# Queries' projection handed out within the recurrence, and the output projection's recurrent half as float32 products

## The chip, the cores and the metric

The kernel runs on one NeuronCore of a Trainium2 chip. The metric is the device time of one execution in microseconds, as the median of the runs shown. Five instruction streams matter: PE (TensorE's matmuls, with PEld for its weight loads), DVE (VectorE), ACT (ScalarE), POOL (GpSimd) and SP (SyncE, which issues the DMAs). Each executes its own list in order; semaphores join them.

## The reference

One step of a streaming layer, for 1024 new frames of one stream and 16 frames for each of 8 running streams, 1152 rows in all, in 9 tiles of 128 rows. What the change touches is marked.

```python
h = rmsnorm(x, norm_mix)
proj = h @ w_in                                  # 1024 -> xr, gate, q, k, v, qi, ki, wi
xc = causal_conv(xr, ...)                        # 4 taps
r, i = sigmoid(xc @ w_rg + b_rg), sigmoid(xc @ w_ig + b_ig)      # 8 blocks of 64
a = exp(-8 * r * softplus(-lru_lambda))
hs = scan(h_t = a_t * h_{t-1} + sqrt(1 - a_t^2) * i_t * xc_t)    # the recurrence, 512 wide
y_a = hs * gelu(gate)
q = rope(rmsnorm(q per head, q_norm), pos)       # moved: 8 heads of 64
k = rope(rmsnorm(k per head, k_norm), pos)
# indexer: scores of qi, ki; top 256 keys of each row; attention over these -> y_b (512 wide)
x = x + concat(y_a, y_b) @ w_out                 # changed: y_a's half, rows 0 to 511 of w_out
hf = rmsnorm(x, norm_ffn)
x = x + (silu(gate part) * up part) @ w_ffn_out
```

All inputs and outputs are float32.

## The kernel before

The class `Kernel` writes the whole program in a chain of phases: norm of `x` with keys and values; indexer; recurrence (`lru`); queries' projection (`q_proj`); recurrent half of the output projection (`out_tile` with the key "wa"); attention; attention half of the output projection ("wb"); feed-forward.

*How products are made.* Most products are made in the type `fp32r`. For the sake of precision an operand is split there into a high and a low part (`split`, or `hi` and `lo`), and `mm3` issues three fast matmuls, high by high, high by low and low by high. `mm4` (L210) issues one true float32 matmul on unsplit operands; the trace shows it as two records of a weight load and a matmul each. The recurrence uses `mm4` for its convolution (`taps` by `xp`, four products added up) and its gates (`bd` by `xc`). All other projections use `mm3` (`mm`, L205).

*Order of the work.* Every piece is a Python generator, a "stream". `run` (L93) steps through `width` streams at a time in the order given, and besides through "side" streams, whenever its model of the engines' clocks says they are due. What comes out is an order for each engine; a scheduler behind it moves instructions once more, so the order of the program differs in many places whenever anything changes. All operations of DVE, ACT and POOL are recorded in one helper, L66, and are told apart by their tiles.

*The recurrence* goes through four columns of 128 channels. For each column `lru_main` projects the input (24 matmuls of 384 columns for each of three thirds of the rows), ACT copies it to `xp`, PE convolves it, ACT copies it to `xc`, PE makes the gates, ACT and DVE (`ti`, `tt`, `tr`) make the coefficients and DVE scans. `lru_gate` projects the column's gelu gate, and POOL multiplies it into `yF`, which holds `y_a` transposed, channel by row, in float32. Beside this the top-k search of the indexer runs as a side stream on DVE (`tk_cand`, `tk_cnt`, `jk`) and ACT (`jk`, passes over scores with a sum).

*Weights.* One stream, `loader`, loads weights in a list's order: DMA into one of two `raw` buffers, then a split into slots of 4 KB a partition in the pool `wr`; there are 8 slots (`SLOTS`). The recurrence's weights come first (two slots for each of eight, alternately main and gate, split on POOL), then two halves of the queries' weights (four slots each), then four rows of 128 of `w_out` ("wa"), the first two in slots and the others in spare room, each split by ACT and POOL (`load_wout`).

*Queries* (`q_tile`, L1197 on): a tile is 128 rows by half of the 512 columns, 24 matmuls of 256 columns; 18 tiles. ACT copies PSUM to `qn` and squares it head by head with a sum (`sq`, four instructions and four reads of the accumulator); then `rope`: DVE `qn` by `tab`, POOL `rp` twice, DVE adds. Nine rotation tables, multiplied by the gain on POOL, serve both halves. This phase begins when all streams of the recurrence have been handed out.

*Recurrent half of the output projection*: `out_prep` splits `yF` tile by tile into `rest` (ACT high, POOL low), `out_tile` loads `x` into `acc`, makes 24 matmuls of 512 columns for each of 9 tiles, and DVE adds PSUM into `acc`. As side streams, `k_rope` rotates the keys (`kn`, one table and one transpose for each tile) and `q_norm` scales the queries (POOL, `qss`).

Of the kernel before, what the change touches and what calls it, by code (L numbers as in the profile page):

```python
# [19 lines left out]
D = 1024  # L20
# [61 lines left out]
class Kernel:  # L82
# [10 lines left out]
    def run(self, streams, width, side=(), carry=()):  # L93
# [4 lines left out]
        act = list(carry)  # L98
# [6 lines left out]
        while todo or act:  # L105
            while todo and len(act) < width:
                act.append([self.clock, todo.pop()])
            self.clock = max([self.clock] + [b - self.QUEUE for b in self.busy.values()])
            for x in list(side):
                if due(x) <= self.clock:  # L110
                    lat = self.step(x[1])
                    if lat is None:
                        side.remove(x)
                    else:
                        x[0] = self.clock + lat
            x = next((a for a in act if a[0] <= self.clock), None)
            if x is None:
                x = min(act, key=lambda a: a[0])
                t = min([x[0]] + [due(a) for a in side])
                if t < x[0]:  # L120
                    self.clock = max(self.clock, t)
                    continue
                self.clock = x[0]
            self.pe0 = self.pe
            lat = next(x[1], None)
            self.clock = self.now()
            self.pe0 = self.pe
            if lat is None:
                act.remove(x)
            else:  # L130
                x[0] = self.clock + lat
# [132 lines left out]
    def build(self, upto=99):  # L264
# [61 lines left out]
        if upto < 3:  # L326
            return close()
        self.fence()
# [45 lines left out]
        with tc.tile_pool(name="wob", bufs=2, side=R) as tp:  # L374
# [3 lines left out]
            self.run([self.out_tile(i, "wb", tp, False) for i in range(NT)] + [self.ffn_start()], self.W_OUT,  # L378
                     [self.out_prep(False)] + side + [self.ffn_first()])
# [9 lines left out]
    YS_LO = ('pool', 'dve')  # L389
    C_FIRST = 2  # L390
# [9 lines left out]
    WA_HE = 'act'  # L400
# [3 lines left out]
    BD = 2  # L404
# [15 lines left out]
    def loader(self):  # L420
        I = self.I
        jobs = [("qi", 8, lambda n: self.load_512(1792, n))]
        jobs += [(("lru", n), 2, lambda n, c=c, n_=n: self.load_cols128(I["w_in"], c, n, self.LRU_HE[n_])) for n, c in enumerate(self.LRU_COLS)]
        jobs += [(("q", k), 4, lambda n, k=k: self.load_cols256(1024 + 256 * k, n)) for k in range(2)]
        jobs += [(("wa", c), 2 if c < 2 else 0, lambda n, c=c: self.load_wout([(0, c * 128, 128)], n, self.WA_HE, self.WA_LO[c]))
                 for c in range(4)]
# [601 lines left out]
    def lru_main(self, n, c, lp):  # L1028
# [14 lines left out]
        taps = lp.tile([128, 4, 128], F32, tag="taps", name="taps", bufs=2)  # L1043
# [148 lines left out]
    def q_proj(self, tp):  # L1192
        gq = self.load_g(tp, self.I["q_norm"], "gq")
        self.n_q, self.qtab = 0, {}
        return [self.q_tile(i, half, tp, gq) for half in range(2) for i in range(NT)]

    def q_tile(self, i, half, tp, gq):  # L1197
# [3 lines left out]
        if not half:  # L1201
            self.qtab[i] = self.tables(tp, i, gq, NT)
# [19 lines left out]
        self.rope(x, x, self.qtab[i], 4, tp)  # L1222
# [54 lines left out]
    WA_LO = ('pool', 'pool', 'pool', 'pool')  # L1277

    def load_wout(self, parts, n, he="act", le="pool"):

        t = self.raw.tile([128, D], F32, tag="raw", name="raw")
        for p0, r0, m in parts:
            self.nc.sync.dma_start(t[p0:p0 + m], self.I["w_out"][r0:r0 + m, :])
        ws = []
        yield from self.claim(n)
        while not n and self.spare is None:
            yield 0.3
        for q in range(2):
            w = self.wslot([2, 512]) if n else self.spare.pop(0).rearrange("p (x n) -> p x n", x=2)
            self.split(w, t[:, q * 512:(q + 1) * 512], he, le)  # L1290
            ws.append(w)
            yield 1.0
        return ws
# [21 lines left out]
    def out_prep(self, first):  # L1315

        self.ys = {}
        if first:

            while self.n_q < NT + 3:  # L1320
                yield 0.3
            self.rest = self.hblk.tile([128, 3 * D], F32R, tag="h", name="rest")
            acc = self.hblk.tile([128, 3, D], F32, tag="h", name="acc")
            self.acc = [acc[:, i] for i in range(3)]

            while self.n_q < NT + 6:
                yield 0.3
            self.smr = self.hblk.tile([128, 3 * D], F32R, tag="h", name="smr")
            self.spare = [self.smr[:, k * 1024:(k + 1) * 1024] for k in range(3)] + [self.rest[:, 2048:3072]]
        for i in range(NT):  # L1330
# [6 lines left out]
            self.lo(ys[:, 1], src, ys[:, 0], self.YS_LO[0 if first else 1])  # L1337
# [3 lines left out]
    def out_tile(self, i, key, tp, first):  # L1341
        nc = self.nc
        if first:
            nc.sync.dma_start(self.acc[i], self.x_src(i))
# [4 lines left out]
        early = first and i < self.C_FIRST  # L1349
        pos = [self.ps(), self.ps()] if early else [None, None]  # L1350
        for c in range(4) if early else ():
            w, = yield from self.wait_w((key, c))
            for q in range(2):
                self.mm3(pos[q], ys[:, 0, c, :], ys[:, 1, c, :], w[q][:, 0, :], w[q][:, 1, :], c == 0, c == 3)
            yield 0.0
        if first:
            w = yield from self.wait_w(*((key, c) for c in range(4)))
            if i == NT - 1:
                self.wused -= 4
        for q in range(2):  # L1360
            if not first:
                u, v = yield from self.wait_w((key, q, 0), (key, q, 2))
                if q and i >= NT - 2:

                    self.half_b += 1
                    while self.half_b < 2:
                        yield 0.2
            po = pos[q]
            if po is None:
                po = self.ps()  # L1370
                for c in range(4):
                    wc = w[c][q] if first else (u + v)[c]
                    self.mm3(po, ys[:, 0, c, :], ys[:, 1, c, :], wc[:, 0, :], wc[:, 1, :], c == 0, c == 3)
# [5 lines left out]
        if not first:  # L1379
            xs = tp.tile([128, D], F32, tag="xs", name="xs", bufs=3)  # L1380
            yield from self.norm_T(self.acc[i], xs, self.gf, self.hf[i // 3], (i % 3) * 128, tp)
            self.hf_done.add(i)
# [367 lines left out]
```

## Time and profile before

| | us |
|---|---|
| median of 3 runs (1585.16 to 1586.07) | 1585.86 |
| the profiled execution, its own time | 1582.82 |
| its span in the trace | 1580.7 |
| norm, keys, values | 0 to 76 |
| indexer | 76 to 186.5 |
| recurrence | 186.5 to 396.5 |
| queries' projection | 396.5 to 449.5 |
| recurrent half of the output projection | 449.5 to 513.3 |
| attention | to about 720 |
| its half of the output projection, feed-forward | to 1580 |

| | busy us | share |
|---|---|---|
| PE | 1477.3 | 93% |
| DVE | 886.4 | 56% |
| ACT | 624.4 | 39% |
| POOL | 288.7 | 18% |

The mean granted clock of TensorE is 0.969. The stages' ends are read from PE's timeline, at the first matmul of a stage. The chain of waits gives PE 72% of the span and DVE 15%. A row of the timeline gives start, length, engine, line, operation, tiles, shape and count of the merged instructions, and in brackets the engine's idle time before it and what ended it. Line numbers are those of the kernel before; in the changed kernel L205, L210 and L215 are L207, L212 and L217.

### The profile page before, as it was taken

To read this page: it belongs to the slowest core of one execution; us is meant where nothing else is said; L and a number is where in the kernel's file an instruction comes from. 1 tells how busy PE (TensorE), PEld (TensorE's weight loads), DVE (VectorE), ACT (ScalarE), POOL (GpSimd) and SP (SyncE) were. 2 spreads that over 40 slices of the span, in tenths; PEclk is the share of its full clock that TensorE was granted. 3 is DMA by queue.
4 is the path that set the end of the run, shared out by engine and by line. 5 is a ranking of instruction groups with operands and counts; after the bars stand their busy time and mean duration, and the time that the engine had idled before them with its cause. 6 is when DMAs were issued, how large, how long until landed. Compare 5 with 4: busy or idle time off the path is not lost.

```text
span 1580.7 us, 21030 instructions
## 1 busy us (share of the span) xinstructions
PE 1477.3 (93%) x7858; PEld 1335.3 (84%) x7858; DVE 886.4 (56%) x1909; ACT 624.4 (39%) x1484; POOL 288.7 (18%) x433
## 2 busy tenths in 40 slices
PE   6899898875989899999999999999999999999998
PEld 6777676764977688888999999999898989898987
DVE  7656899998676887768424242423333242424143
ACT  5447967867631987755312120202020202121100
POOL 5424223227484444400000000000000000000000
PEclk7999899988999899999999999999999999999999
DMA  7211110100140001120302020202020202111002
GB/s 241 66 32 42 35 29 16 29 14 14 44 156 0 8 14 47 48 67 28 94 14 67 14 75 6 80 1 80 1 80 0 81 18 63 30 51 52 29 1 120
DMA packets 93798, 74.66 MB, mean 47 GB/s; under 512 B 13236, under 2 KB 84532, under 8 KB 93696
## 3 DMA queue, kind: packets, MB, share of 16 engines
q1 hardware_dynamic: 93696, 73.32, 15.5%
q8 instruction: 62, 1.02, 0.3%
q14 instruction: 40, 0.33, 0.1%
HBM read 67.03 MB, written 6.27 MB: 46 GB/s over the span
## 4 chain that ended last, share of the span: by engine, by line
PE 72%; DVE 15%; ACT 5%; POOL 3%; issue 3%; DMA 1%; SPq 0%; POOLq 0%; ACTq 0%; DVEq 0%
PE ps L205 67%; DVE jk L66 7%; PE ps L215 3%; DVE tk_cand L66 2%; ACT jk L66 1%; DVE tr L66 1%; POOL rp L66 1%; PE ps L210 1%; DVE ti L66 1%; POOL qn L66 1%; DVE s L66 1%; ACT qeo L66 1%; ACT m L66 1%; ACT relu L66 0%; DMA tab<-in_rope_dram 0%
## 5 line engine op out<-in xcount | busy, mean ns | idle before, releaser
L205 PE MATMUL ps<-hf,w 128*128 128x384 f32 x2556 | 460.6, 338 | 0.0
L205 PEld LDWEIGHTS ps<-hf,w 128*128 128x128 f32 x2556 | 451.5, 187 | 0.8
L205 PE MATMUL ps<-w,a 128*128 128x512 f32 x999 | 239.1, 390 | 0.0
L66 DVE TENSOR_TENSOR acc<-ps,acc 128x512 f32<-128x512 f32 x234 | 161.3, 690 | 134.4 <-PE ps L205 133.9
L205 PEld LDWEIGHTS ps<-w,a 128*128 128x128 f32 x999 | 187.3, 188 | 40.1
L66 ACT ACTIVATE w<-raw 128x512 fp32r<-128x512 f32 x128 | 77.8, 630 | 303.0 <-PE ps L205 220.9
L66 DVE TENSOR_TENSOR sg<-ps,sg 128x384 f32<-128x384 f32 x66 | 36.7, 557 | 276.4 <-PE ps L205 275.9
L66 DVE TENSOR_TENSOR w<-raw,w 128x512 fp32r<-128x512 f32 x116 | 76.8, 687 | 87.4 <-ACT w L66 87.2
L66 ACT ACTIVATE jk<-s,tk_cand 128x384 bf16<-128x384 f32 (+3 forms) x128 | 99.4, 776 | 61.8 <-DVE tk_cand L66 53.0
L66 ACT ACTIVATE a<-sg 128x384 fp32r<-128x384 f32 x66 | 34.5, 523 | 217.9 <-DVE sg L66 217.9
L205 PE MATMUL ps<-hf,rest 128*128 128x384 f32 x612 | 114.5, 334 | 0.0
L205 PE MATMUL ps<-h,w 128*128 128x384 f32 x576 | 108.7, 347 | 0.5 <-ACT relu L66 0.5
L205 PEld LDWEIGHTS ps<-hf,rest 128*128 128x128 f32 x612 | 106.9, 188 | 0.2
L205 PEld LDWEIGHTS ps<-h,w 128*128 128x128 f32 x576 | 102.3, 190 | 4.7 <-ACT relu L66 0.6
L205 PE MATMUL ps<-w,h 128*128 128x256 f32 (+1 forms) x600 | 94.6, 314 | 0.6 <-DVE to L66 0.6
L205 PE MATMUL ps<-w,rest 128*128 128x512 f32 x324 | 83.0, 406 | 8.2 <-POOL rest L66 8.0
L205 PEld LDWEIGHTS ps<-w,h 128*128 128x128 f32 x600 | 82.2, 188 | 7.3 <-DVE to L66 0.9
L205 PEld LDWEIGHTS ps<-w,rest 128*128 128x128 f32 x324 | 61.3, 194 | 22.7 <-POOL rest L66 8.9
L66 ACT ACTIVATE sg<-ps 128x384 f32<-128x384 f32 x66 | 32.1, 486 | 122.0 <-PE ps L205 122.0
L210 PE MATMUL ps<-xp,taps 128*128 128x384 f32 (+2 forms) x128 | 44.5, 504 | 37.7 <-ACT xp L66 37.7
L210 PEld LDWEIGHTS ps<-xp,taps 128*128 128x128 f32 x128 | 26.7, 231 | 51.7 <-issue 43.8
L66 POOL TENSOR_SCALAR m<-m,mx 128x128 f32<-128x128 f32 (+7 forms) x64 | 47.6, 752 | 68.5 <-DVE mx L66 61.7
(261 smaller groups left out, 2185.2 us busy)
## 6 DMA issues: line engine op xcount, KB each, us to landing
raw<-in_w_ffn_in_dram SPq DMA_DIRECT2D x44, 512.0 KB, 4.9
raw<-in_w_ffn_out_dram SPq DMA_DIRECT2D x22, 512.0 KB, 3.5
raw<-in_w_in_dram SPq DMA_DIRECT2D x16, 512.0 KB, 3.8
out_dram<-acc SPq DMA_DIRECT2D x9, 512.0 KB, 2.6
x<-in_x_prompt_dram SPq DMA_DIRECT2D x8, 512.0 KB
acc<-in_x_prompt_dram SPq DMA_DIRECT2D x8, 512.0 KB, 9.1
tab<-in_rope_dram SPq DMA_DIRECT2D x34, 64.0 KB, 1.8
raw<-in_w_out_dram SPq DMA_DIRECT2D x4, 512.0 KB, 3.5
```

The costliest lines, as they stand in the source:

```text
L66: return f(*args, **kw)
L205: self.nc.tensor.matmul(out, lhsT, rhs, start=start, stop=stop)
L210: self.nc.tensor.matmul(out, lhsT, rhs, start=start, stop=stop)
L215: self.nc.tensor.transpose(out, in_, self.ident[0:n, 0:n])
```

## The change

- `run` takes a list `back` in place of `carry`: streams that are stepped only when no stream of the phase is ready, two of them at a time. `q_proj`'s 18 streams are made before the recurrence and passed as `back`; what is left of them runs in the queries' phase. Their memory now exists beside the recurrence's, and for that `bd` and `taps` have one buffer each instead of two, and the rotation tables three buffers instead of nine, so that each of the 18 tiles loads and multiplies its own.
- The loader brings the first half of the queries' weights after the third of the recurrence's eight weights, the second half after the eighth. The first half holds four of the eight slots until its ninth tile.
- The recurrent half of the output projection multiplies in float32: `load_wa` loads 128 rows of `w_out` into one slot, unsplit; `out_tile_a` issues `mm4` on `yF` and `wa`, 8 products of 512 columns for each of 9 tiles, 72 in place of 216 fast ones. The splits of `yF` (9 on ACT, 9 on POOL) and of these weights (8 and 8) are gone. `out_prep` is left to the attention half; its allocations are in `out_room`.

```diff
-    def run(self, streams, width, side=(), carry=()):
+    def run(self, streams, width, side=(), back=()):
...
-            x = next((a for a in act if a[0] <= self.clock), None)
+            x = next((a for a in act + list(back[:2]) if a[0] <= self.clock), None)
             if x is None:
-                x = min(act, key=lambda a: a[0])
+                x = min(act + list(back[:2]), key=lambda a: a[0])
...
-        with tc.tile_pool(name="lru", bufs=1, side=R) as tp:
-            self.phase = 1
-            side = self.run(self.lru(tp), 3, [self.lru_prep(tp)] + side)
...
         with tc.tile_pool(name="tq", bufs=2, side=R) as tp:
+            queries = [[self.clock, g] for g in self.q_proj(tp)]
+            with tc.tile_pool(name="lru", bufs=1, side=R) as lp:
+                self.phase = 1
+                side = self.run(self.lru(lp), 3, [self.lru_prep(lp)] + side, queries)
             self.phase = 2
-            prep, lo = self.out_prep(True), self.lru_out()
-            side = [x for x in self.run(self.q_proj(tp), 3, [prep, lo] + side) if x is not prep]
+            prep, lo = self.out_room(), self.lru_out()
+            side = [x for x in self.run([g for _, g in queries], 3, [prep, lo] + side) if x is not prep]
...
-            side = self.run([self.out_tile(i, "wa", None, True) for i in range(NT)], 2, [prep] + side + [kr, qr])
+            side = self.run([self.out_tile_a(i) for i in range(NT)], 2, [prep] + side + [kr, qr])
...
-    BD = 2
+    BD = 1
...
-        jobs += [(("wa", c), 2 if c < 2 else 0, lambda n, c=c: self.load_wout([(0, c * 128, 128)], n, self.WA_HE, self.WA_LO[c]))
-                 for c in range(4)]
+        lru = [(("lru", n), 2, lambda n, c=c, n_=n: self.load_cols128(I["w_in"], c, n, self.LRU_HE[n_])) for n, c in enumerate(self.LRU_COLS)]
+        q = [(("q", k), 4, lambda n, k=k: self.load_cols256(1024 + 256 * k, n)) for k in range(2)]
+        jobs += lru[:3] + q[:1] + lru[3:] + q[1:]
+        jobs += [(("wa", c), 1, lambda n, c=c: self.load_wa(c)) for c in range(4)]
...
-        taps = lp.tile([128, 4, 128], F32, tag="taps", name="taps", bufs=2)
+        taps = lp.tile([128, 4, 128], F32, tag="taps", name="taps", bufs=1)
...
-        if not half:
-            self.qtab[i] = self.tables(tp, i, gq, NT)
+        tab = self.tables(tp, i, gq, 3)
...
+    def load_wa(self, c):
+
+        yield from self.claim(1)
+        w = self.wr.tile([128, D], F32, tag="w", name="wa")
+        self.nc.sync.dma_start(w, self.I["w_out"][c * 128:(c + 1) * 128, :])
+        return w
...
+    def out_tile_a(self, i):
+
+        nc = self.nc
+        nc.sync.dma_start(self.acc[i], self.x_src(i))
+        w = []
+        pos = [self.ps(), self.ps()]
+        for c in range(4):
+            w += yield from self.wait_w(("wa", c))
+            for q in range(2):
+                self.mm4(pos[q], self.yF[:, c, i * 128:(i + 1) * 128], w[c][:, q * 512:(q + 1) * 512], c == 0, c == 3)
+            yield 0.0
+        if i == NT - 1:
+            self.wused -= 4
+        for q in range(2):
+            a = self.acc[i][:, q * 512:(q + 1) * 512]
+            nc.vector.tensor_tensor(a, pos[q], a, op=ALU.add)
+            yield 0.4 if q else 0.0
```

More of the change, by code (lines that the diff above doesn't have):

```diff
@@ L90, in __init__ @@
         self.nc = Engines(tc.nc, self)
-    def run(self, streams, width, side=(), carry=()):
+    def run(self, streams, width, side=(), back=()):
         todo = list(streams)[::-1]
-        act = list(carry)
+        act = []
         side = self.side = [[self.clock, g] for g in side]
@@ L128, in run @@
             if lat is None:
-                act.remove(x)
+                (act if any(x is a for a in act) else back).remove(x)
             else:
@@ L377, in build @@
             self.half_b, self.hf_done, self.w1_first, self.first_ps = 0, set(), [], {}
-            self.run([self.out_tile(i, "wb", tp, False) for i in range(NT)] + [self.ffn_start()], self.W_OUT,
-                     [self.out_prep(False)] + side + [self.ffn_first()])
+            self.run([self.out_tile(i, tp) for i in range(NT)] + [self.ffn_start()], self.W_OUT,
+                     [self.out_prep()] + side + [self.ffn_first()])
         yst.close()
@@ L388 @@
     LO_LAT = 15.0
-    YS_LO = ('pool', 'dve')
-    C_FIRST = 2
     WARM = 16
@@ L399 @@
     EXP_EARLY = False
-    WA_HE = 'act'
     WB_HE = 'act'
@@ L1193, in q_proj @@
         gq = self.load_g(tp, self.I["q_norm"], "gq")
-        self.n_q, self.qtab = 0, {}
+        self.n_q = 0
         return [self.q_tile(i, half, tp, gq) for half in range(2) for i in range(NT)]
@@ L1221, in q_tile @@
         x = x.rearrange("p (h d) -> p h d", h=4)
-        self.rope(x, x, self.qtab[i], 4, tp)
+        self.rope(x, x, tab, 4, tp)
     def q_norm(self, tp):
@@ L1274, in k_rope @@
             yield 2.0
[L1277 to L1293, printed above, removed]
+    def load_wa(self, c):
[3 more added lines that the diff above has]
+        return w
     def load_wb(self, q, c0, n):
@@ L1313, in x_src, with out_room, out_prep @@
                 else self.I["x_sample"].rearrange("b t d -> (b t) d"))
-    def out_prep(self, first):
-        self.ys = {}
[L1318 to L1329, printed above, removed]
+    def out_room(self):
+        while self.n_q < NT + 3:
+            yield 0.3
+        self.rest = self.hblk.tile([128, 3 * D], F32R, tag="h", name="rest")
+        acc = self.hblk.tile([128, 3, D], F32, tag="h", name="acc")
+        self.acc = [acc[:, i] for i in range(3)]
+        while self.n_q < NT + 6:
+            yield 0.3
+        self.smr = self.hblk.tile([128, 3 * D], F32R, tag="h", name="smr")
+    def out_prep(self):
+        self.ys = {}
         for i in range(NT):
@@ L1336, in out_prep, with out_tile @@
             self.hi(ys[:, 0], src)
-            self.lo(ys[:, 1], src, ys[:, 0], self.YS_LO[0 if first else 1])
+            self.lo(ys[:, 1], src, ys[:, 0], "dve")
             self.ys[i] = ys, self.end()
             yield 0.3
-    def out_tile(self, i, key, tp, first):
+    def out_tile_a(self, i):
         nc = self.nc
-        if first:
-            nc.sync.dma_start(self.acc[i], self.x_src(i))
+        nc.sync.dma_start(self.acc[i], self.x_src(i))
[12 more added lines that the diff above has]
+            yield 0.4 if q else 0.0
+    def out_tile(self, i, tp):
+        nc = self.nc
         while i not in self.ys:
@@ L1348, in out_tile @@
         yield from self.until(t)
[L1349 to L1359, printed above, removed]
-        for q in range(2):
[L1361 to L1373, printed above, removed]
+        for q in range(2):
+            u, v = yield from self.wait_w(("wb", q, 0), ("wb", q, 2))
+            if q and i >= NT - 2:
+                self.half_b += 1
+                while self.half_b < 2:
+                    yield 0.2
+            po = self.ps()
+            for c in range(4):
+                wc = (u + v)[c]
+                self.mm3(po, ys[:, 0, c, :], ys[:, 1, c, :], wc[:, 0, :], wc[:, 1, :], c == 0, c == 3)
             a = self.acc[i][:, q * 512:(q + 1) * 512]
@@ L1378, in out_tile @@
             yield 0.4 if q else 0.0
[L1379 to L1382, printed above, removed]
+        xs = tp.tile([128, D], F32, tag="xs", name="xs", bufs=3)
+        yield from self.norm_T(self.acc[i], xs, self.gf, self.hf[i // 3], (i % 3) * 128, tp)
+        self.hf_done.add(i)
     def attn(self, i, kv, tp):
```

5 lines of the change are left out of this document (removed).

## The prediction

> **What bounds the kernel now.** I read the table of windows first, cut where the stages change (recurrence 186.5 to 396.5 us, queries' projection to 449.5, recurrent half of the output projection to about 513). The columns are the stretch, its length, busy time of PE, PEld, DVE, ACT and POOL, granted clock, DMA share, GB/s.
>
> ```profile
> 186.50:396.50 210.00, 163.18 (x754) 138.56 (x753) 198.43 (x493) 152.87 (x324) 68.98 (x90) 0.91 0.08 22
> 396.50:449.50 53.00, 52.04 (x438) 51.48 (x437) 34.33 (x62) 33.95 (x179) 33.15 (x47) 1.00 0.31 101
> 449.50:515.00 65.50, 56.84 (x239) 45.30 (x238) 45.08 (x91) 13.52 (x45) 40.01 (x47) 0.92 0.12 40
> 760.00:1580.00 820.00, 816.28 (x4285) 767.14 (x4283) 285.97 (x453) 136.03 (x255) 0.00 (x0) 1.00 0.15 45
> ```
>
> Three stages with three limits: in the recurrence DVE works 198.4 of 210 us (its own scans and the top-k that runs beside them) and PE idles 47; the queries' projection is PE alone, at full clock; in the output half PE has gaps and a clock of 0.92. From 760 us PE is full, and the change leaves that part alone. The waits of the recurrence name the gaps (total, times, longest):
>
> ```profile
> ACT jk L66 <- DVE tk_cand L66: 48.3, 18, 5.6
> PE ps L210 <- ACT xp L66: 37.7, 9, 8.9
> PE ps L210 <- ACT xc L66: 8.6, 3, 3.8
> ```
>
> PE's convolution needs ACT's copy `xp`; ACT executes in order, and its top-k pass (`jk`) waits for DVE. So 46.3 us of PE are free there, in pieces of up to 8.9 us. PE's timeline shows the last pieces, then the queries without a gap (start, length, operation, idle before it):
>
> ```profile
> 355.78 2.74 PE L210 MATMUL ps<-xp,taps 128*128 128x384 f32 x8
> 358.07 4.62 PE L205 MATMUL ps<-h,w 128*128 128x384 f32 x24
> 370.77 4.64 PE L210 MATMUL ps<-xp,taps 128*128 128x384 f32 x8 [8.08 <-ACT xp L66]
> ...
> 388.64 3.38 PE L210 MATMUL ps<-xp,taps 128*128 128x256 f32 x8 [7.77 <-ACT xp L66]
> ...
> 395.45 1.56 PE L210 MATMUL ps<-xc,bd 128*128 128x384 f32 x4 [1.25 <-ACT xc L66]
> 396.55 17.42 PE L205 MATMUL ps<-w,h 128*128 128x256 f32 x144
> 413.81 0.49 PE L215 MATMUL ps<-ident,tail 128*36 128x128 f32 x3
> ```
>
> And the output half, with two waits for POOL's split of `yF` and matmuls at half speed behind them:
>
> ```profile
> 449.55 2.92 PE L205 MATMUL ps<-w,rest 128*128 128x512 f32 x12
> 452.31 2.23 PE L205 MATMUL ps<-smr,rest 128*128 128x512 f32 x9
> ...
> 464.46 2.93 PE L205 MATMUL ps<-w,rest 128*128 128x512 f32 x6 [3.71 <-POOL rest L66]
> 467.19 2.76 PE L205 MATMUL ps<-smr,rest 128*128 128x512 f32 x6
> 469.75 0.41 PE L215 MATMUL ps<-ident,kn 128*128 128x128 f32 x1
> ...
> 477.26 2.93 PE L205 MATMUL ps<-w,rest 128*128 128x512 f32 x6 [4.33 <-POOL rest L66]
> 479.99 1.68 PE L205 MATMUL ps<-smr,rest 128*128 128x512 f32 x6
> ...
> 494.21 1.55 PE L205 MATMUL ps<-smr,rest 128*128 128x512 f32 x6
> 495.60 1.55 PE L205 MATMUL ps<-w,rest 128*128 128x512 f32 x6
> ...
> 513.34 1.04 PE L215 MATMUL ps<-ident,qn 128*128 128x128 f32 x8
> ```
>
> **Step 1: queries that leave their own stage.** PE's order around the end of the recurrence, before (`taps` is a convolution, `bd` a gate, `w,h` with 256 columns a query tile of two such rows):
>
> ```order
> L210 MATMUL ps<-xp,taps 128x384 x4
> L210 MATMUL ps<-xc,bd 128x384 x2
> L205 MATMUL ps<-h_0_99,w 128x384 x12
> L205 MATMUL ps<-h_1_100,w 128x384 x12
> L210 MATMUL ps<-xp,taps 128x256 x4
> L210 MATMUL ps<-xc,bd 128x384 x2
> L210 MATMUL ps<-xp,taps 128x128 x4
> L210 MATMUL ps<-xc,bd 128x384 x2
> L205 MATMUL ps<-w,h_0_95 128x256 x12
> L205 MATMUL ps<-w,h_1_96 128x256 x12
> ```
>
> The same place after:
>
> ```order
> L207 MATMUL ps<-h_0_99,w 128x384 x12
> L207 MATMUL ps<-h_1_100,w 128x384 x12
> L207 MATMUL ps<-w,h_0_97 128x256 x12
> L207 MATMUL ps<-w,h_1_98 128x256 x12
> L212 MATMUL ps<-xp,taps 128x256 x4
> L212 MATMUL ps<-xp,taps 128x128 x4
> L212 MATMUL ps<-xc,bd 128x384 x2
> L207 MATMUL ps<-w,h_0_97 128x256 x12
> L207 MATMUL ps<-w,h_1_98 128x256 x12
> L212 MATMUL ps<-xc,bd 128x384 x2
> ```
>
> A query tile now stands ahead of the last convolution, where PE waited 7.77 us, and another ahead of the last gates. In the whole recurrence I count six such tiles (two in the first column, one in each of the next two, two in the last); the other twelve follow the last gates. 144 matmuls took 413.81 - 396.55 = 17.26 us, so a tile of 24 takes 2.88 us, and six leave their stage: -17.3 us. Their cover is the 46.3 us of PE's waits; if it were gone they would cost the 17.3 us again.
>
> **Step 2: what they bring into the recurrence.** Each tile issues these on the other engines (busy, mean ns; `tab` and `rp` rows serve the rotation):
>
> ```profile
> L66 DVE TENSOR_TENSOR qn<-qn,tab 128x256 f32<-128x256 f32 x18 | 15.1, 836 | 15.1 <-POOL rp L66 9.7 <-ACT sq L66 5.4
> L66 DVE TENSOR_TENSOR qn<-qn,rp 128x256 f32<-128x256 f32 x18 | 12.8, 714 | 0.5
> L66 ACT ACTIVATE sq<-ps 128x64 bf16<-128x64 f32 x72 | 15.6, 262 | 0.0
> L66 ACT ACTIVATION_READ_ACCUMULATOR sq<-ps 128x1 f32 x72 | 15.4, 246 | 0.0
> L66 ACT ACTIVATE qn<-ps 128x256 f32<-128x256 f32 x18 | 6.7, 406 | 12.7 <-DVE tk_cnt L66 9.7 <-PE ps L205 2.9
> L66 POOL TENSOR_TENSOR rp<-qn,tab 128x128 f32<-128x128 f32 x36 | 19.1, 560 | 1.5 <-DVE qn L66 1.5
> ```
>
> ACT: 0.41 + 4 x (0.26 + 0.25) = 2.4 us a tile, 14.6 for six, in 57 idle us; POOL: 12 x 0.56 = 6.7 us, in 141. DVE is the engine that sets the end: 6 x (0.836 + 0.714) = 9.3 us on top of 198.4 gives 207.7. If they fill its idle time (11.6 us) wholly, the stage ends 2.3 us earlier; if none of it, 9.3 later. I take +3.5, the middle. DVE and POOL also get into each other's way: the same DVE instruction takes 0.67 us or 1.52.
>
> ```profile
> 428.17 0.57 DVE L66 TENSOR_TENSOR qn<-qn,rp 128x256 f32<-128x256 f32 x1
> 428.67 1.52 DVE L66 TENSOR_TENSOR qn<-qn,tab 128x256 f32<-128x256 f32 x1
> ...
> 430.22 0.57 DVE L66 TENSOR_TENSOR qn<-qn,rp 128x256 f32<-128x256 f32 x1
> ```
>
> The row means above hold that already for the rotations; if each of the twelve `rp` held up one more DVE instruction of the recurrence for its whole 0.56 us, the end would come 6.7 us later still, +16.0 at worst. The Trainium skill's page "SBUF — State Buffer" (section "Who interferes with whom" and the section on the two sides) has the rule that speaks against moving this work here: the pair of ports that the two share is held for a whole instruction, and the other engine stands still. The 0.57 and 1.52 us agree with it; by the rule alone the term would be nearer +10 than +3.5.
>
> Their loads move too, on SP's queue (one row for all tables):
>
> ```profile
> tab<-in_rope_dram SPq DMA_DIRECT2D x34, 64.0 KB, 1.8
> ```
>
> Nine more tables are loaded and multiplied by the gain on POOL, and with three buffers a load waits for DVE's rotation three tiles back. Behind it on SP's queue stand the gates' `bd` loads (one buffer now, so that they also wait for the last gates of the column before, as `taps` on ACT waits for its last convolution), the next `raw` loads, and later the four `wa` loads. I cost all this at nothing: a load of 1.8 us for `bd` lies beside a third's projection (4.62 us) and convolution, and the `wa` loads beside the twelve tiles. If that cover is gone it is the first rival's case.
>
> **Step 3: the output half in float32.** Before, 216 matmuls of 512 columns; 6 start 1.39 us apart (494.21 to 495.60), 0.232 us each, 50.0 us; their last one ends 0.16 us after the next could start. The stage runs 513.34 - 449.55 = 63.8 us: 50.0, 8.0 of waits, 3.9 lost behind them (2.73, 2.56 and 2.73 us in place of 1.39), and 1.9 of transposes. In PE's order this stage opened so, three products of split halves for each:
>
> ```order
> L205 MATMUL ps<-w,rest 128x512 x12
> L205 MATMUL ps<-smr,rest 128x512 x9
> L205 MATMUL ps<-rest 128x512 x3
> L205 MATMUL ps<-w,rest 128x512 x12
> L205 MATMUL ps<-smr,rest 128x512 x9
> ```
>
> After, behind the last query tile:
>
> ```order
> L207 MATMUL ps<-w,h_1_100 128x256 x12
> L212 MATMUL ps<-wa,yF 128x512 x16
> L217 MATMUL ps<-ident,kn 128x128
> L212 MATMUL ps<-wa,yF 128x512 x5
> L217 MATMUL ps<-ident,kn 128x128
> L212 MATMUL ps<-wa,yF 128x512 x7
> ```
>
> It is 72 products straight from `yF` and `wa`, and the keys' transposes between them. No float32 product of 512 columns is in the trace. The nearest is the convolution's, 384 columns, where the trace has two records a product: four took 2.74 us, less 0.16 for the last one's end 0.645 each, and by columns 512/384 x 0.645 = 0.86 us, an estimate. 72 x 0.86 = 61.9, with the 1.9 of transposes 63.8: nothing gained or lost, the waits and the half speed being paid out in longer products. Bounds: 2.74/4 unshortened gives 0.913 and +3.8; from start to next start (355.78 to 358.07) 0.573, hence 0.763, and -7. The Trainium skill ("TensorE: Matmul & The Clock Gate", section "Back-to-back issue gap") has sustained matmuls of 512 columns at about 131 ns; the 0.232 us here contradict that. By it four passes would be 0.52 us and the stage 24 us shorter.
>
> What leaves the other engines here, 9 and 8 instructions of these kinds on POOL and as many on ACT, hid beside PE except in the 8 us:
>
> ```profile
> L66 POOL TENSOR_TENSOR rest<-yF,rest 128x512 fp32r<-128x512 f32 x9 | 12.0, 1337 | 6.3 <-ACT rest L66 6.2
> L66 POOL TENSOR_TENSOR w<-raw,w 128x512 fp32r<-128x512 f32 x36 | 49.7, 1387 | 6.4 <-ACT w L66 5.4
> ```
>
> **Step 4: the head.** The keys' rotation was scheduled into the first 76 us and now, since its memory is in use later, stands in the output half. PE waited once there behind it:
>
> ```profile
> 40.55 0.37 DVE L66 TENSOR_TENSOR kn<-kn,tab 128x128 f32<-128x128 f32 x1 [0.57 <-POOL rp L66]
> ...
> 47.41 0.40 PE L215 MATMUL ps<-ident,kr 128*64 128x128 f32 x1 [3.68 <-DVE kr L66]
> ```
>
> I take -1.5 (0 to -3.7). In the output half these few instructions have the DVE's idle time as cover: it was busy 34.3 + 45.1 of 118.5 us from 396.5 to 515.
>
> **Sum.** -17.3 + 3.5 + 0 - 1.5 = -15.3 us: the profiled execution's 1582.8 would be 1567.5, the median of 1585.9, 3.0 above it, 1570.6. A difference under 0.2%, 3.2 us, counts as none.
>
> **Rivals.** *Weights come too late (slower).* The first half of the queries' weights holds four of eight slots all through, and the recurrence has four left instead of eight; a column's first weight can be split only when the column before gives its slots back. The two halves of a weight cost POOL 2 x (0.68 + 1.39) = 4.1 us, and the load 3.8 if it waits too.
>
> ```profile
> L66 POOL TENSOR_SCALAR w<-raw 128x512 fp32r<-128x512 f32 x24 | 16.1, 676 | 16.1 <-PE ps L205 15.6 <-DMA raw<-in_w_in_dram 0.2
> raw<-in_w_in_dram SPq DMA_DIRECT2D x16, 512.0 KB, 3.8
> ```
>
> Three columns at 7.9 us are +23.7, so +8.4 in all: 1594. It decides from 5.1 us a column on. For it: POOL already waited 15.6 us for PE to free slots. Against: between a column's last projection and the next column stand the 24 matmuls of a last third (4.6 us), a convolution (2.7) and a query tile (2.9), some 10 us. 0.14.
>
> *DVE eats it.* The worst of step 2, +16.0: 1583.1, within 0.2% or just faster. For it: DVE has only 5% left. Against: PE's waits sit in the last column, where DVE too was not full. 0.15, about half of it "same".
>
> *The page's 131 ns.* -24: 1546. The 0.232 us speaks against it. 0.02.
>
> *It does not do what it says.* Six of eighteen tiles are inside by the order, so most of it is done only in name; that is in the sum. If those six sit where PE didn't wait, -17.3 is lost and +2.0 is left: 1588, no change. 0.02.
>
> **How the numbers follow.** The forecast has 0.67; its own terms reach from -28.1 (-2.3 and -7) to -4.2 (+9.3, +3.8 and no gain in the head), 1558 to 1582. Faster: 0.67 + 0.02 for the page + 0.08 of DVE's case, 0.77; same: 0.07 + 0.02, 0.09; slower 0.14. The range, 1557 to 1584, takes in DVE's case and leaves out the late weights and the page's.
>
> **What would show it.** Right: the last gates on PE at 394 to 410 us, twelve tiles in some 36 us behind them, the float32 stage at 62 to 66 us without waits for POOL and full clock, first query transposes of the attention near 498. Wrong: PE waiting in columns two to four for POOL's `w`; a product of 512 columns far from 0.86 us; DVE's first `acc` addition far behind PE's first output product.

## The result and the profile after

The changed kernel takes 1571.74 us in the median of 4 runs (1571.28 to 1572.55) against 1585.96 for the kernel before in the same series: 14.2 us less by the medians, ratio 0.9914, 95% interval 0.9898 to 0.9929. Its profiled execution took 1571.56 us with a span of 1569.8; the one of before, 1582.82, lies 3 us below its own median, so that the two traces differ by 11 us where the medians differ by 14. Everything below that compares stages goes by the traces.

The same cuts in both traces, at PE's first instruction of a stage (columns as in the prediction: stretch, length, busy PE, PEld, DVE, ACT, POOL, clock, DMA share, GB/s). The attention ends here at PE's first product of its half of the output projection (686.53 and 675.63 us). Before: recurrence, queries, output half, attention, rest:

```profile
186.22:396.55 210.33, 163.51 (x757) 138.87 (x757) 198.71 (x493) 153.20 (x324) 68.98 (x90) 0.91 0.08 22
396.55:449.55 53.00, 52.04 (x438) 51.50 (x437) 34.38 (x62) 33.90 (x179) 33.20 (x47) 1.00 0.31 101
449.55:513.34 63.79, 55.75 (x231) 44.46 (x230) 43.47 (x85) 11.97 (x39) 38.35 (x45) 0.92 0.12 40
513.34:686.53 173.19, 160.27 (x991) 138.50 (x989) 139.87 (x425) 136.07 (x334) 71.59 (x97) 0.95 0.10 27
686.53:1580.70 894.17, 889.59 (x4666) 830.47 (x4664) 342.25 (x569) 175.70 (x329) 0.00 (x0) 1.00 0.15 47
```

After:

```profile
184.31:402.08 217.77, 182.37 (x902) 158.65 (x901) 204.87 (x522) 162.94 (x384) 74.90 (x107) 0.90 0.08 21
402.08:436.73 34.65, 34.65 (x295) 34.48 (x294) 24.52 (x49) 19.92 (x111) 21.20 (x38) 1.00 0.47 172
436.73:508.99 72.26, 66.12 (x160) 28.67 (x159) 50.16 (x106) 10.47 (x43) 40.75 (x66) 0.98 0.17 53
508.99:675.63 166.64, 154.67 (x991) 135.18 (x989) 136.52 (x413) 132.91 (x324) 70.01 (x96) 0.98 0.10 28
675.63:1569.80 894.17, 889.53 (x4666) 830.43 (x4664) 342.49 (x569) 175.67 (x329) 0.00 (x0) 1.00 0.15 47
```

By length: recurrence +7.4, queries -18.4, output half +8.5, attention -6.6, the rest 0.0; the recurrence starts 1.9 us earlier. The sum is -11.0; without the rounding it is the 10.9 us between the spans. The queries' gain is there; the recurrence and the output half give most of it back, and the attention, which the change doesn't touch, gains.

The place where the prediction's order rows were, on PE (start, length, operation, idle before):

```profile
387.05 2.99 PE L207 MATMUL ps<-w,h 128*128 128x256 f32 x24
392.95 4.27 PE L212 MATMUL ps<-xp,taps 128*128 128x256 f32 x16 [2.91 <-ACT xp L66]
397.06 1.45 PE L212 MATMUL ps<-xc,bd 128*128 128x384 f32 x4
398.06 3.19 PE L207 MATMUL ps<-w,h 128*128 128x256 f32 x24
401.08 1.45 PE L212 MATMUL ps<-xc,bd 128*128 128x384 f32 x4
402.08 25.89 PE L207 MATMUL ps<-w,h 128*128 128x256 f32 x216
...
428.16 8.73 PE L207 MATMUL ps<-w,h 128*128 128x256 f32 x72
```

The first tile stands in front of the last convolution, and 2.91 us of the wait for `xp` are left of 7.77: there most of it is covered. 216 + 72 matmuls, twelve tiles, follow the last gates.

The float32 stage on PE, its first half and two of its steady pieces:

```profile
436.73 8.26 PE L212 MATMUL ps<-wa,yF 128*128 128x512 f32 x18
445.15 6.28 PE L212 MATMUL ps<-wa,yF 128*128 128x512 f32 x14 [0.16 <-DVE jk L66]
452.42 0.30 PE L217 MATMUL ps<-ident,kn 128*128 128x128 f32 x1 [0.99 <-DVE jk L66]
452.67 2.81 PE L212 MATMUL ps<-wa,yF 128*128 128x512 f32 x6
460.37 3.52 PE L212 MATMUL ps<-wa,yF 128*128 128x512 f32 x4 [4.88 <-DVE acc L66]
...
476.98 0.27 PE L217 MATMUL ps<-ident,kn 128*128 128x128 f32 x1
477.09 7.03 PE L212 MATMUL ps<-wa,yF 128*128 128x512 f32 x16
483.96 0.27 PE L217 MATMUL ps<-ident,kn 128*128 128x128 f32 x1
```

Steady, 16 records or 8 products run from 477.09 to 483.96, 0.859 us a product. None of PE's waits in this stage names POOL any more; all name DVE, 6.0 us in three, and the four records behind the longest take 3.3 us where steady ones take 1.7. The chain of waits (start, length, what) alternates between POOL and DVE up to 445 us, goes through DVE alone up to the first addition to `acc`, and through PE from there; its last part:

```profile
453.27 2.01 DVE qn L66 x2
455.29 0.72 DVE kn L66
457.39 1.42 DVE ps L66
458.81 0.91 DVE s L66 x2
459.71 0.61 DVE acc L66
460.37 3.52 PE ps L212 x4
464.10 6.06 PE ps L212 x14
```

In front of the first `acc` in DVE's order stand the queries' and keys' rotations (`qn`, `kn`) and the masks of the top-k (`ps`, `s`). That addition starts 22.9 us behind PE's first output product, against 13.5 before (463.07 and 449.55 us).

### The profile page after: what moved, and what is told of

Read it like the earlier page. It is cut to its first block, busy times and chain, and to the rows that moved or that the text cites. A ratio compares the mean times of both kernels' runs of the same rounds, so it can differ in the third digit from the quotient of the medians.

```text
span 1569.8 us, 20865 instructions
## 1 busy us (share of the span) xinstructions
PE 1484.3 (95%) x7786; PEld 1319.3 (84%) x7786; DVE 881.0 (56%) x1909; ACT 614.5 (39%) x1467; POOL 269.5 (17%) x425
## 4 chain that ended last, share of the span: by engine, by line
PE 72%; DVE 14%; ACT 6%; issue 4%; POOL 2%; DMA 1%; SPq 0%; POOLq 0%; ACTq 0%; DVEq 0%
PE ps L207 65%; DVE jk L66 6%; PE ps L212 4%; PE ps L217 3%; DVE tk_cand L66 2%; ACT jk L66 2%; DVE tr L66 1%; POOL rp L66 1%; DVE s L66 1%; DVE ti L66 1%; DVE qn L66 1%; ACT L66 1%; ACT m L66 0%; DMA x<-in_x_prompt_dram 0%; DMA acc<-in_x_prompt_dram 0%
## 5 line engine op out<-in xcount | busy, mean ns | idle before, releaser
L207 PEld LDWEIGHTS ps<-hf,rest 128*128 128x128 f32 x612 | 106.9, 188 | 0.2
L212 PE MATMUL ps<-wa,yF 128*128 128x512 f32 x144 | 65.5, 607 | 5.2 <-DVE acc L66 4.9
L212 PEld LDWEIGHTS ps<-wa,yF 128*128 128x128 f32 x144 | 26.9, 194 | 39.3 <-issue 30.6
```

The costliest lines, as they stand in the source:

```text
L207: self.nc.tensor.matmul(out, lhsT, rhs, start=start, stop=stop)
L212: self.nc.tensor.matmul(out, lhsT, rhs, start=start, stop=stop)
```

## The experiments

Lengths of the stages in all traces, cut as above, in us ("tail" is the end of the recurrence to the attention's first transposes):

| kernel | recurrence | queries | output half | tail | attention | ratio to before, 95% interval |
|---|---|---|---|---|---|---|
| before | 210.3 | 53.0 | 63.8 | 116.8 | 173.2 | |
| after | 217.8 | 34.7 | 72.3 | 106.9 | 166.6 | 0.9914 (0.9898 to 0.9929) |
| f32_only | 211.4 | 52.8 | 64.4 | 117.2 | 169.4 | 0.9980 (0.9971 to 0.9989) |
| queries_only | 217.7 | 34.6 | 71.9 | 106.6 | 173.4 | 0.9955 (0.9940 to 0.9970) |
| no_x_load | 217.8 | 34.7 | 72.4 | 107.0 | 168.3 | 0.9924 (0.9911 to 0.9937) |
| late_rope | 218.1 | 34.7 | 79.6 | 114.3 | 171.0 | 0.9979 (0.9969 to 0.9988) |
| no_handout | 210.6 | 56.1 | 64.7 | 120.8 | 170.0 | 0.9975 (0.9961 to 0.9988) |
| no_handout_8slots | 215.7 | 56.2 | 63.2 | 119.4 | 166.7 | 0.9987 (0.9977 to 0.9997) |
| late_sq | 222.6 | 33.1 | 74.6 | 107.8 | 168.0 | 0.9946 (0.9928 to 0.9965) |
| act_copy | 216.6 | 34.7 | 68.3 | 103.0 | 168.3 | 1.0003 (0.9994 to 1.0012) |
| thin_tiles | 213.2 | 32.2 | 74.9 | 107.1 | 167.3 | 0.9900 (0.9882 to 0.9919) |
| act_stage6 | 219.6 | 34.7 | 72.1 | 106.8 | 170.3 | 0.9931 (0.9915 to 0.9946) |
| more_tiles | 240.3 | 14.8 | 71.3 | 86.1 | 168.7 | 0.9945 (0.9931 to 0.9958) |
| more_tiles_stage | 243.2 | 14.8 | 79.1 | 93.9 | 169.3 | 0.9984 (0.9974 to 0.9994) |

The rest takes 894 us in all of them but `act_copy` (912).

Each row's lengths come from one execution, the ratio from all runs of the kernel. They don't always agree: the executions of `act_stage6` run from 1570.21 to 1577.06 us, and the traced one of `more_tiles_stage`, 1586.85, lies 5.0 above its median. Five kernels with the same six tiles inside (after, queries_only, no_x_load, act_copy, act_stage6) have recurrences of 216.6 to 219.6 us. A difference of 3 us between two rows of one column is therefore not shown to come from the edit.

### One part at a time: f32_only, queries_only

`f32_only` puts the recurrence, its buffers, the loader's order and the nine tables back:

```diff
-    BD = 1
+    BD = 2
...
-        jobs += lru[:3] + q[:1] + lru[3:] + q[1:]
+        jobs += lru + q
...
-                side = self.run(self.lru(lp), 3, [self.lru_prep(lp)] + side, queries)
+            side = self.run(self.lru(tp), 3, [self.lru_prep(tp)] + side)
```

> The float32 half alone, queries' projection and recurrence as before. Theory (72 products at 0.86 us, worth the 216 fast ones with their two waits; what the stage lost in the changed kernel comes from loads that delay DVE there, not from the products): the stage from the first output product to the attention's first query transposes is 62 to 66 us (63.8 before), the median 1583 to 1588, no difference. Rival (the float32 form is dearer as such, also by what it makes DVE wait): stage 70 us or more as in the changed kernel (72.3), median 1592 or more.

The stage took 64.4 us, with one wait of 0.9 for DVE: as the theory had it, the products are worth the split ones. The median is 1581.66, 0.2% below before, clear of 1 by its interval: slightly better than expected. Where these 4 us lie the trace doesn't show: its execution took 1582.70, no less than the 1582.82 of before, with an attention 3.8 us shorter and a recurrence that starts 2.4 us later.

`queries_only` puts `load_wout`, `out_prep` and the split products back into the changed kernel.

> The queries handed out within the recurrence, the output half in split fast products as before. Theory (the gain is the queries' stage, 53.0 to 34.7 us, less some 7 us by which the recurrence grows): median 1571 to 1578. Rival (the two parts need each other: POOL has the queries' and the output weights to split at once, and the output half waits for it): stage of the output half over 72 us, median 1580 or more.

1578.15 us: between the two cases. The recurrence and the queries' stage are those of the changed kernel to 0.1 us; the output half took 71.9 us, and PE's timeline has the rival's wait:

```profile
449.18 0.84 PE L207 MATMUL ps<-rest 128*128 128x512 f32 x3
460.30 2.93 PE L207 MATMUL ps<-w,rest 128*128 128x512 f32 x6 [10.28 <-POOL rest L66]
463.02 2.55 PE L207 MATMUL ps<-smr,rest 128*128 128x512 f32 x6
```

So either form of the output half loses some 8 us when the queries' stage ahead of it is 18 us shorter, by waits that name POOL in the one and DVE in the other. (`f32_only` also leaves the keys' rotations in the head, as before. That alone is not the difference: `no_handout`, below, has them moved and all queries in their stage, and its output half takes 64.7 us.) DVE's first addition is early here, at 449.19 us; in POOL's order seven scalings of the queries (`qn` by `qss`, 7.7 us) stand ahead of the split that PE waits for. The two parts by themselves give -0.2% and -0.45%, together -0.86%; by the traces, what the float32 half adds to the queries lies in the attention (173.4 to 166.6).

### What holds PE in the output half: no_x_load, act_copy, act_stage6

POOL's timeline of the changed kernel shows a wait for a keys' table whose DMA stood behind the 512 KB loads of `x`, and DVE waits for POOL behind it:

```profile
431.42 0.46 POOL L66 TENSOR_TENSOR tab<-tab,gk 128x128 f32<-128x128 f32 x1 [5.38 <-DMA acc<-in_x_prompt_dram]
```

```profile
433.14 0.53 DVE L66 TENSOR_TENSOR qn<-qn,tab 128x256 f32<-128x256 f32 x1 [6.03 <-POOL rp L66]
```

That made the first theory. `no_x_load` takes these loads away (x is left out of the result):

```diff
-        nc.sync.dma_start(self.acc[i], self.x_src(i))
...
-            nc.vector.tensor_tensor(a, pos[q], a, op=ALU.add)
+            nc.vector.tensor_copy(a, pos[q])
```

> The changed kernel without the nine loads of x into acc; DVE copies the first half's products into acc, so that x is left out of the output. Theory (those 512 KB loads stand ahead of the 64 KB rotation tables on the DMA queues; POOL waits for a table, DVE for POOL, and the additions to acc behind them come late, so that PE runs out of PSUM banks): PE's 4.9 us wait for DVE in the output half goes, the stage shrinks from 72.3 to 63 to 66 us, median 1562 to 1567. Rival (DVE is late because it has too much to do there): stage still 70 us or more, median within 3 us of the changed kernel's 1571.7.

The theory fell. The 6.03 us wait was gone, the stage took 72.4 us all the same (median 1573.73), and PE waited as long as before, 5.9 us against 6.0, now put down to another DVE instruction:

```profile
459.31 3.78 PE L212 MATMUL ps<-wa,yF 128*128 128x512 f32 x4 [5.94 <-DVE tk_cnt L66]
```

DVE's first copy to `acc` came at 458.58 us, in the changed kernel the first addition at 459.64. That wait for the table did not set the time. From the recurrence's end to the first addition DVE's busy time is nearly the same before and after, in a stretch that is 9 us shorter:

```profile
396.55:463.07 66.52, 63.24 (x486) 60.33 (x484) 46.23 (x84) 36.73 (x191) 44.41 (x66) 1.00 0.36 119
```

```profile
402.08:459.64 57.56, 52.15 (x333) 41.40 (x331) 46.96 (x89) 22.01 (x123) 41.54 (x67) 1.00 0.45 156
```

The two sums hold different work. The queries' rotations on DVE fall from 26.9 to 16.4 us, since the tiles inside the recurrence have theirs behind them; the keys' rotations, which the change moved here from the head, bring 3.6; and the masks rise from 2.6 to 14.7, because four of them stand ahead of the first addition instead of one. How much of the late addition is owed to that order no run here tests by itself.

In `no_x_load`, to just behind the start of the first copy:

```profile
402.65:459.30 56.65, 50.72 (x331) 41.19 (x329) 49.21 (x94) 22.19 (x123) 40.82 (x70) 0.99 0.20 64
```

DVE does more there ahead of its first copy, five first steps of the keys' rotations (`kn` by `tab`) where the changed kernel has three: the order moved too. And it is still idle for 7.4 us, against 10.6, most of it in shorter waits for POOL. So its work fills most of this stretch but not all of it.

`act_copy` takes the PSUM banks off DVE: ACT copies, and `x` is loaded and added by POOL in the attention's half of the output projection.

```diff
-        nc.sync.dma_start(self.acc[i], self.x_src(i))
...
-            nc.vector.tensor_tensor(a, pos[q], a, op=ALU.add)
+            nc.scalar.activation(a, pos[q], AF.Copy)
...
+        xin = tp.tile([128, D], F32, tag="xin", name="xin", bufs=2)
+        nc.sync.dma_start(xin, self.x_src(i))
+        self.pool_tt(self.acc[i], self.acc[i], xin, ALU.add)
```

> The changed kernel with the first half's products copied from PSUM to acc by ACT, which has 9 of 68 us to do there, and x loaded and added by POOL in the attention half of the output projection. Theory (PE's waits in the float32 stage are for DVE, which has more work in its order up to there than time): the stage shrinks from 72.3 to 63 to 65 us; median 1563 to 1566 if the attention starts as much earlier, 1568 to 1571 if DVE's masks then hold up the attention. Rival (not DVE but the keys' chain of POOL, DVE and the transposes among the products holds PE): stage 70 us or more.

The stage shrank to 68.3 us, half of what was expected; PE still waited three times, 1.42, 1.16 and 1.58 us, all put down to DVE. The attention's half of the output projection and the feed-forward then took 18 us more (median 1586.03). The loads of `x` were issued only from 682.4 us on; POOL waited 24.0 us in seven waits for them, DVE for POOL, and PE stood idle for 10.1 and 3.9 us behind that (start, length, DVE, idle before):

```profile
691.14 1.29 DVE L66 TENSOR_TENSOR acc<-ps,acc 128x512 f32<-128x512 f32 x2 [4.21 <-POOL acc L66]
```

`act_stage6` leaves `x` where it is and gives ACT six staging tiles, from which DVE adds:

```diff
-            nc.vector.tensor_tensor(a, pos[q], a, op=ALU.add)
+            st = self.woa.tile([128, 512], F32, tag="st", name="st", bufs=6)
+            nc.scalar.activation(st, pos[q], AF.Copy)
+            nc.vector.tensor_tensor(a, st, a, op=ALU.add)
```

> The changed kernel, where ACT first copies a half's product from PSUM into one of six staging tiles and DVE adds that to acc. Theory (DVE has some 46 to 50 us of work ahead of its first addition, and PE has shortened the time before it; what PE lacks is a free PSUM bank, not the sum): the float32 stage shrinks from 72.3 to 66 to 69 us, as in the run in which ACT copied and x came later, without that run's loss in the second half; median 1566 to 1569. Rival (the masks and the keys then hold up the attention by as much): attention's score products start no earlier than 511 us, median 1570 or more.

No gain: 72.1 us, and a median of 1575.55, as the rival had it. PE waited 1.14 us for DVE before the fifth half tile and 4.25 us behind the sixth:

```profile
453.18 3.67 PE L212 MATMUL ps<-wa,yF 128*128 128x512 f32 x8 [1.14 <-DVE jk L66]
...
464.65 6.37 PE L212 MATMUL ps<-wa,yF 128*128 128x512 f32 x8 [4.25 <-DVE jk L66]
```

Both waits name `jk`, the mask instructions that read PSUM themselves (`jk` from `ps`); that banks held by the masks were what PE lacked here is not excluded.

With six tiles handed out, the tail is 106.6 to 107.1 us in five kernels (after, queries_only, no_x_load, thin_tiles, act_stage6), whatever the form of the output half, whether a table is late, and though PE has less to do in `thin_tiles`; only ACT's copies took 4 us off it (`act_copy`, 103.0), and in `late_rope`, which puts six rotations behind the recurrence, it is 114.3. PE's own part of it is some 99 us (34.7 and 63.8 or 64.4). So what holds the tail is work of the other engines behind the recurrence that PE's shorter stage no longer covers. That it is DVE's alone is not shown: `late_rope` puts off 10.1 us of POOL's work with DVE's, PE's longest wait names POOL in `queries_only`, and DVE itself waits for POOL before its first addition (9.6 us in the changed kernel). The two engines work in turns on the rotations. Only `act_copy` relieves one of them alone: it takes the additions off DVE, and gains half of the loss.

### What lengthened the recurrence: late_rope, no_handout, no_handout_8slots, late_sq, thin_tiles

`late_rope` lets the tiles' matmuls and ACT's copies stand in the recurrence, but ties the gain of their tables to the last scan:

```diff
+            one = self.qn[:, NP, 511:512]
+            nc.vector.tensor_scalar(one, self.tail[:, 3, 27:28], 0.0, 1.0, op0=ALU.mult, op1=ALU.add)
...
+            nc.gpsimd.tensor_scalar(g2, g2, one, 0.0, op0=ALU.mult, op1=ALU.add)
```

> The changed kernel with the rotations of the query tiles made to wait for the end of the recurrence (the gain of the rotation tables is multiplied by one that depends on the last scan); their matmuls and ACT's copies stay inside. Theory (the recurrence grew from 209.4 to 216.8 us because DVE, its limit, got six rotations of 1.55 us): last gates on PE at 393 to 396 us instead of 401; later stages may lose what is put off. Rival (it grew by the halved weight slots and the single buffers of bd and taps, or by ACT's added copies): last gates at 400 us or later.

The prediction's own mechanism found no support here: the last gates come at 400.93 us. DVE is busy 7.1 us less in the recurrence than in the changed kernel (204.9), and the stage takes as long (median 1582.23):

```profile
183.93:402.03 218.10, 178.96 (x901) 155.50 (x901) 197.73 (x494) 159.85 (x374) 64.76 (x90) 0.93 0.08 20
```

`no_handout` leaves the loader's order and the single buffers and hands out nothing; the other gives the eight slots back.

```diff
-                side = self.run(self.lru(lp), 3, [self.lru_prep(lp)] + side, queries)
+                side = self.run(self.lru(lp), 3, [self.lru_prep(lp)] + side)
```

> The changed kernel with no query tile handed out before the recurrence ends; its loader order (four weight slots for the recurrence) and its single buffers of bd and taps stay. Three theories on why the recurrence grew from 209.4 to 216.8 us though the rotations turned out not to be the cause. Memory (fewer slots, single buffers): it still takes 215 to 218 us. The tiles themselves (their 2.9 us on PE ahead of a convolution, or 2.4 us on ACT ahead of its copies): 208 to 211 us. Both: in between. The queries' stage is 52 to 53 us again either way.

> As no_handout, and the loader order of before, so that the recurrence has all eight slots; bd and taps keep one buffer. If memory is the cause and it is the slots: recurrence 208 to 211 us. If it is the single buffers: as long as in no_handout, 215 to 218. If the tiles are the cause: 208 to 211 in both.

210.6 us: neither the four slots nor the single buffers cost anything, and the rival that the prediction gave to the slower side has no ground. The second run is a miss for all three theories: 215.7 us with more slots. What differs is the loader's order and the order of instructions that the scheduler makes from it; PE is idle for 53.6 us there against 44.3. So a change of order without any tile is worth 5 us in this stage, and a difference of that size in one trace proves little. `late_rope` came out 5 us later than its theory allowed, so it doesn't rule DVE's rotations out for certain.

`late_sq` is `late_rope` with the squares of the tiles put off too (scale from the same last scan).

> As late_rope, and the squares of the handed-out tiles (four ACT instructions and four reads of the accumulator a tile, 2.0 us) are made to wait for the end of the recurrence too, from the copy in SBUF; only matmuls and one ACT copy of 0.4 us a tile stay inside. If ACT's added work stretches the recurrence: 209 to 212 us against 217.2 in late_rope. If PE's tiles or memory do: 215 us or more.

222.6 us: putting the squares off shortened nothing. But a seventh tile stood inside the recurrence here (926 matmul records against 901), so that the two runs differ by more than the squares, and this run alone doesn't clear them.

`thin_tiles` cuts a tile's matmuls inside the recurrence to a third (the low parts are left out) and leaves the tile's work on the other engines:

```diff
+            if self.phase == 1:
+                self.mm(pq[:, :256], self.h_lhs(i, d, 0), ww[:, d % 2, 0, :], d == 0, d == ND - 1)
+                self.pe += 2 * 256 / 2400.0
+                continue
```

> The changed kernel, where a query tile inside the recurrence makes only its high-by-high matmuls, 8 instead of 24 (the low parts are left out of those six tiles); the order of the rest stays nearly the same. Theory (the recurrence grew by 7.2 us because six tiles of 2.9 us stand on PE, less than half of it out of hearing of the chain that sets the end): at a third of the matmuls the recurrence takes 210 to 213 us instead of 217.8. Rival (not PE's time, but the place and the small instructions that a tile brings to the other engines): 216 us or more.

213.2 us, just above the theory's range, with DVE and POOL as busy as in the changed kernel to 2 us (203.2 and 74.8) and ACT busy 6 us less. (Three more tiles that were handed out in this form stand behind the recurrence, which is why the queries' stage is shorter too.) With 17.3 us of query matmuls inside the recurrence takes 217.8, with 5.8 us 213.2, with none 210.6: about 0.4 us for each microsecond of them. PE's own time, of which three fifths are hidden, fits these three best. It is not proved: `no_handout_8slots` has no tile inside and takes 215.7, more than `thin_tiles`, and `late_sq` with seven tiles takes 4 us more than this rate gives.

### More tiles inside: more_tiles, more_tiles_stage

```diff
-    LRU_LAT = 3.0
+    LRU_LAT = 8.0
```

> The changed kernel with LRU_LAT, the planner's idea of the latency behind a convolution, at 8 instead of 3 us: by the order 13 of 18 tiles stand inside the recurrence. If a tile inside costs the recurrence 1.2 us as the six did: recurrence 225 to 227 us, queries' stage 14 to 16 us, so 10 to 12 us earlier at the output half's start. DVE's work behind the recurrence then decides: it still has 37 to 45 us ahead of its first addition, so the output half loses 5 to 15 us of that in waits; median 1563 to 1571. Rival (the recurrence is at DVE's limit and each tile more costs its full 2.9 us): recurrence 236 us or more, median over 1571.

> Both, 13 tiles inside and ACT's staging. If PE's waits in the output half are for PSUM banks: 4 to 6 us under more_tiles, median 1558 to 1566. Rival (DVE's total work up to the attention is the limit, wherever its additions stand): within 2 us of the better of the two alone.

240.3 us, 3.2 for each of seven more tiles: the rival's case in its size, and all that the queries' stage saved (19.9) was lost. But DVE was not at its limit, and the median is 1575.92:

```profile
184.96:425.22 240.26, 198.38 (x1070) 175.84 (x1069) 215.60 (x544) 170.77 (x447) 85.17 (x128) 0.91 0.12 35
```

24.7 us of DVE and 41.9 of PE are idle there, against 12.9 and 35.4 in the changed kernel. On balance the tiles filled no gaps. The setting moves gates too, so how much of it is the tiles' is open. The tail, 86.1 us, is 21 shorter than with six tiles, so it is no fixed length: the rotations of seven more tiles stand ahead of it. With the staging tiles it was slower still (1581.88 us), which neither expectation had. No variant beat the changed kernel with the whole computation in it.

## Why the prediction was right

It gave 1570.6 us, in a range of 1557 to 1584, and 1571.7 was measured. Of its signs, the last gates (401.08 us) and the twelve tiles (34.65 us) came as said; the float32 stage (72.3 instead of 62 to 66 us) and the attention's first transposes (508.99 instead of 498) did not, and one that it gave for being wrong appeared, DVE's first addition to `acc` 22.9 us behind PE's first output product. Step by step:

- **Queries that leave their stage**: -17.3 forecast, -18.4 measured, the six tiles and the small waits of before. Right.
- **The recurrence**: +3.5 forecast, +7.4 measured, inside the range given. The size was fair; the reason, "DVE is the engine that sets the end" and six rotations lengthen it, found no support. With the rotations put off it took as long; with a third of the tiles' matmuls it took 4.6 us less. The lower bound of -2.3 was no bound either: work that fills idle time can't end a stage earlier, so 0 was the least, and the middle 4.7. The 46.3 us of PE's waits were taken for cover, but only 11.4 us of PE's idle time were filled (46.8 to 35.4, at 18.9 us more of busy time).
- **The float32 half**: 0 forecast, +8.5 measured, outside the bounds of -7 to +3.8. The price was right, 0.859 us a product against an estimate of 0.86, and by itself the stage took 64.4 us. What failed is the statement that DVE's idle time covers what moves here ("busy 34.3 + 45.1 of 118.5 us"): a mean over two stages, one of which the change itself shortens by 18 us. This was the rival of a late DVE at another place, behind the recurrence instead of in it, with POOL's share in it left open above. The steady row contradicts the 131 ns of the Trainium skill's page "TensorE: Matmul & The Clock Gate" (section "Back-to-back issue gap") and agrees with the warm formula that the section gives for an isolated gap: a quarter of 0.859 us is 0.215, where N/2.4 + 2.5 gives 216 ns for 512 columns. That a true float32 product is four passes stands in the Trainium skill's page "FP8 and Floating Point Precision" (section "TensorE Precision Notes"); the trace shows two records a product, not the passes themselves, and its time fits four.
- **The head**: -1.5 forecast, -1.9 measured at the recurrence's start. Right: the wait of 3.68 us is gone, and PE's last transpose of `kr` comes at 72.80 us instead of 76.04, and the stretch to the recurrence gives 1.3 of that back.
- **Not in the sum**: the attention, -6.6. Two pieces can be placed. One is at its front, where the granted clock of the first 20 us is higher and DVE's first `qeo` is waited for 1.74 us instead of 2.98. Before and after:

```profile
513.34:533.34 20.00, 14.59 (x72) 12.00 (x71) 17.30 (x70) 18.39 (x54) 7.26 (x17) 0.74 0.05 15
508.99:528.99 20.00, 16.29 (x95) 14.64 (x94) 17.39 (x70) 18.87 (x54) 6.82 (x18) 0.83 0.05 14
```

  The third set of query transposes comes 16.5 us into the stage instead of 21.0. This goes with the float32 half: in all twelve kernels that have it, that set comes at 16.2 to 17.2 us, at a clock of 0.83, and in the two without it at 21.0, at 0.74. Why the clock is higher behind it no run here settles. The other piece is near the end, where PE waits 3.1 us for POOL in both and the matmuls behind run at a clock of 0.59 for 6 us before and at 1.00 after; it does not go with the float32 half, as the clock of that end varies from 0.85 to 1.00 among the kernels that have it.

So a term too good by 8.5 us and one by 3.9 met an unforeseen 6.6, a surplus of 1.5 in the first and fourth steps, and 3 us by which the profiled execution of before lies under its median. Part of the hit is luck.

## What to carry to other kernels

When a stage is shortened, ask first what another engine did during it: here 18 us fewer on PE left work of DVE and POOL without cover (DVE's alone 47 us), and nearly half the gain came back as waits one stage later. A wait that names a DMA, removed, may only show the next one; in five kernels with different named waits the tail stayed at 107 us. Idle time of an engine is cover only where the filler stands in front of a wait, so price it by the gap at that place, not by the stage's sum.

## What the runs showed of the hardware

A float32 product of 512 columns, two records with a weight load each, runs at 0.859 us from start to start, without a gap on PE for its weight loads. Before, DVE's `qn` by `tab` of 128x256 took 0.67 us at 427.47 and 1.52 at 428.67, the second while POOL split a weight (`w` from `raw` and `w`, 1.48 us from 428.42 on). The nine POOL additions of 128x1024 in `act_copy` took 2.45 us on the mean. The start of the attention ran at a granted clock of 0.83 behind float32 products and of 0.74 behind split ones.
